# Turning the gated mixer sum and a quarter of the normed rows by transposing DMAs in a two-layer encoder kernel

## The chip, the cores and the metric

The kernel runs on one core of a Trainium2 chip. The metric is the device time of one launch in microseconds. Before the change it was 1870.2 us, the median of three runs (1869.01 to 1872.32).

## The reference, cut to what matters

Two layers, each a half-step FFN, a gated mixer and a second half-step FFN; a final RMSNorm. D is 1024, there are 512 tokens, the FFN is 2816 wide, everything is float32.

```python
def rms_norm(x, g):
    return x * rsqrt(mean(x * x, -1) + 1e-6) * g
def swiglu(x, w_in, w_out):                       # w_in 1024 x 5632, w_out 2816 x 1024
    g, u = split(x @ w_in, 2)
    return (silu(g) * u) @ w_out
def mixer(h, ...):
    q, k, v, uf, ga, gf = columns_of(h @ w_in)
    y_na = neighbourhood_attention(q, k, v, rpb) @ w_na_out
    y_f = fourier_mix(uf) @ w_f_out               # real part of a 2-D DFT
    g_na, g_f = sigmoid(ga + bias[0]), sigmoid(gf + bias[1])
    return (g_na * y_na + g_f * y_f) @ w_o        # the gated mixer sum, times w_o
for l in range(2):
    x = x + 0.5 * swiglu(rms_norm(x, ffn1_norm[l]), ffn1_w_in[l], ffn1_w_out[l])
    x = x + mixer(rms_norm(x, mix_norm[l]), ...)
    x = x + 0.5 * swiglu(rms_norm(x, ffn2_norm[l]), ffn2_w_in[l], ffn2_w_out[l])
out = rms_norm(x, final_norm)
```

## The kernel before, in words

**Engines.** PE is TensorE, DVE is VectorE, ACT is ScalarE, POOL is GpSimd, SP is SyncE; a queue named after an engine holds the DMAs that this engine issues, in order.

**Products.** Each float32 factor is split into a high and a low part of the multiplying type, and a product is three matmuls per block, high times high, high times low and low times high (`late_low`, L491, L492 and L494). The large products are also cut into 2x2 blocks and formed by Strassen's seven products, which carry the numbers 1 to 7 in the code; sums of blocks are needed on both sides. PE multiplies with the activations as the stationary operand (128 channels on the partitions by 128 tokens), so activations must stand with channels on the partitions: what is computed with tokens on the partitions is turned (transposed) first.

**Weights.** They stream from HBM in pieces (granules) of 128x1024 float32, 512 KB. SP loads a piece into a `raw` buffer (L148). Where Strassen needs a sum of two pieces, it is formed in one of two ways: DVE adds two loaded buffers (L164), or POOL issues a second DMA that accumulates onto the loaded buffer (L150; L196 for a buffer that has been used and becomes the sum). Then ACT copies the high part, `whi` (L191, L186 where the sign is turned), and DVE subtracts for the low part, `wlo` (L194, L187). `whi` and `wlo` have three buffers each. A product asks for its pieces two ahead (`AHEAD`), and loading runs eight pieces ahead of splitting (`FETCH`); in an FFN `raw` has nine buffers of its own, in a mixer its buffers come from the general pool of 23 slots. The order of instructions on each engine is made by a scheduler from the order of the program, except in stretches under `manual_schedule`, where the program's order is kept. Each engine runs its instructions strictly in that order, SP and POOL too.

**FFN.** After the gate and up products come 21 steps (`steps` in `stage_ffn`), each one Strassen product of an activation block with pieces of the out-projection: first product 1 with the three chunks of the inner width (steps 0 to 2), then product 2 (3 to 5), then products 5, 6, 7, 3 of chunk 0 (6 to 9), of chunk 1 and of chunk 2, then product 4. DVE forms the activation sums (`at`, L742) and their low parts (`c5l` and so on, L322); ACT makes the high parts (`c5h`, L321). Products go to PSUM banks `o`; finished ones are added into the residual `x` (`update`, L748).

**How the FFN turns its activations.** `halves` (L676) lets ACT copy the low and the high 16 bits of a 128x1024 float32 block apart into `zs` (two copies, L681); SP then issues a transposing DMA from `zs` to `zt` (L682). `joined` (L687) later lets ACT put the two halves together in `at` (L698). This runs ten times in each FFN, while the gate and up products are being made.

**How the residual rows are turned.** The next block needs the normed rows with channels on the partitions: `Norm.quad(i, j)` turns the quarter of `x` with channels `i*512` and up and tokens `j*256` and up. `quad_high` (L385) issues eight PE transposes of 128x128 float32 into two PSUM banks named `tr` (L396), ACT copies them out in four pieces and multiplies each by its gain, which goes by channel and so by partition (`xr`, L399), then makes the high part `xh` (L400); DVE makes the low part `xl` (L401). In the three FFNs that are not the last one (`late` is false), the quarter (0, 0) is turned in step 6 (L942), when product 2 has been added to it; two more are turned in the step of product 4 with chunk 0.

**The mixer's gated sum.** `gate_block(0, ...)` and `gate_block(1, ...)` (L1374) form the two column halves of the gates by seven products each, in the order 1, 5, 2, 6, 7, 3, 4, with banks `A`, `B` and `C`; ACT copies finished banks out (`snap`, L561, tile `sn`), and `after` is a table of what else is done behind which product. Block 0 leaves the finished gated sum of the first 512 channels in `ga0[0]` and `ga0[1]` (tiles `fs`, 256 tokens each). During block 1, `to_channels(0, ga0, 1)` behind product 5 and `to_channels(0, ga0, 0)` behind product 2 turn these: eight PE transposes each (L1462) into two banks `tr`, two ACT copies to `mq` (L1463). Then come the products with `w_o` ("wA" to "wC"), which read `mq`; the second half of the sum is turned at their start by `to_channels(1, ...)`.

Of the kernel before, what the change touches and what calls it, by code (L numbers as in the profile page):

```python
# [9 lines left out]
F32 = mybir.dt.float32  # L10
# [3 lines left out]
U16 = mybir.dt.uint16  # L14
AF = mybir.ActivationFunctionType
# [3 lines left out]
P = 128  # L19
D = 1024  # L20
T = 512
# [69 lines left out]
def encoder_kernel(  # L91
    ctx: ExitStack, tc: tile.TileContext, xin, xtr, wst, gains, gfin, gbias, bias_in, dft, chan, ident_in, rot, out
):
    nc = tc.nc
    V, S, G, PE = nc.vector, nc.scalar, nc.gpsimd, nc.tensor
# [11 lines left out]
    def nm(s):  # L107
        uid[0] += 1
        return f"{s}_{uid[0]}"

    def slot(dt=F32, s="k", shape=(4, 256)):
        return kp.tile([P, *shape], dt, tag="k", name=nm(s), bufs=23)
# [8 lines left out]
    def pair(s="ps"):  # L121
        return [bank(s), bank(s)]


    x = cp.tile([P, TB, D], F32, tag="x", name="x")
# [193 lines left out]
    def split(hi, lo, src, scale=None):  # L319
        if scale is None:  # L320
            S.activation(hi, src, AF.Copy)  # L321
            V.tensor_tensor(lo, src, hi.bitcast(F32), ALU.subtract)  # L322
            return
        S.activation(hi, src, AF.Copy, scale=scale)
        V.scalar_tensor_tensor(lo, src, scale, hi.bitcast(F32), ALU.mult, ALU.subtract)
# [5 lines left out]
    def rsqrt(ms, n):  # L331
# [6 lines left out]
            V.scalar_tensor_tensor(r, t, 1.5, r, ALU.add, ALU.mult)  # L338
        return r

    class Norm:


# [37 lines left out]

        def quad(self, i, j):
            self.quad_high(i, j)()

        def quad_high(self, i, j):  # L385

# [211 lines left out]
    def stage_ffn(norm, nxt, late):  # L598
# [4 lines left out]
        def at_tile(h, j, c):  # L603
            if (h, j, c) not in at:
                at[h, j, c] = slot(F32, "at")
            return at[h, j, c]
# [17 lines left out]
        raw = norm.raw  # L624
# [17 lines left out]
        acts, steps_of = combos(norm, t4)  # L642
# [6 lines left out]
        if first:  # L649
            for g in range(2):  # L650
                w = ws.next()
# [22 lines left out]
        late_at, turned = [], []  # L674

        def halves(z, j, f0):  # L676

            s, t = slot(U16, "zs", (2, 4, 2, P)), slot(U16, "zt", (2, 4, 256))
            words = z.bitcast(U16).rearrange("p b (q f h) -> p h q b f", q=4, h=2)
            for h in range(2):  # L680
                S.activation(s[:, h], words[:, h], AF.Copy)  # L681
            nc.sync.dma_start_transpose(  # L682
                out=t.rearrange("p h q (b t) -> p (h q b) t", b=2), in_=s.rearrange("p h q b f -> p (h q b f)")
            )
            turned.append((t, j, f0))

        def joined():  # L687

            t, j, f0 = turned.pop(0)
            q = 0  # L690
            while q < 4:
                h, c, i = PLACE[f0 + q]
                n = 1
                while q + n < 4 and PLACE[f0 + q + n] == (h, c, i + n):
                    n += 1
                to = at_tile(h, j, c).bitcast(U16).rearrange("p i (t w) -> p w i t", w=2)
                for w in range(2):
                    S.activation(to[:, w, i : i + n, :], t[:, w, q : q + n, :], AF.Copy)  # L698
                q += n

        def plain_out():
# [161 lines left out]
        for jb in range(0 if first else 1, NB):  # L863
            f0 = 2 + 4 * jb
            if first and jb == 0:
                with tc.manual_schedule(engines={mybir.EngineType.DVE, mybir.EngineType.Activation}):
                    pa = pair("A")
                    product(pa, acts[1], K4, True)
                    for j in range(2):
                        t = snap(pcl[j])  # L870
# [39 lines left out]
        for i, (m, c, _) in enumerate(steps):  # L910
            make(i)
            if i:
                make(i + 1)
            key = {6: 1, 4: 7}.get(m, m)
            if key not in ps:
                ps[key] = pair(f"o{key}")
            if m == 4 and c == 0 and nxt.mix:
                make(i + 2)
                ws.finish_stage()
                swap_pools(1)  # L920
            product(
                ps[key], made.pop(i), list(range(len(CHUNK[0][c]))), c == 0 and m in (1, 2, 3, 5, 7), c == 2,
                m in (4, 6), by_block=late and i == len(steps) - 1,
            )
            if i == 0:
                settle_at()
            if i == 2:
                turned.reverse()
                joined()
            if i == 5:  # L930
                joined()
            if m == 4 and c == 0 and not late:
                with tc.manual_schedule(engines={mybir.EngineType.DVE, mybir.EngineType.Activation}):
                    make(i + 2)
                    nxt.quad(1, 1)
                    if nxt.mix:
                        nxt.low01 = nxt.quad_high(0, 1)
                    else:
                        nxt.quad(0, 1)
            make(i + 2)  # L940
            if i == 6 and not late:
                nxt.quad(0, 0)  # L942
            if m == 4 and c == 1:
                update(ps[1], 1, 0, 1)
            if m == 4 and c == 0 and late:
                gf[0] = slot(F32, "gf", (D,))
                nc.sync.dma_start(out=gf[0], in_=bass.AP(tensor=gfin.tensor, offset=gfin.offset, ap=[[0, P], [1, D]]))
            if c < 2:
                continue
            if m == 1:  # L950
                update(ps[1], 0, 0, -1)
            elif m == 2:
                update(ps[2], 0, 0, 1)
                nxt.squares(0, 0)
            elif m == 5:
                update(ps[5], 0, 1, 1)
                update(ps[5], 1, 1, -1)
            elif m == 6:
                update(ps[1], 1, 1, 1)
            elif m == 7:  # L960
                update(ps[7], 1, 1, 1)
                nxt.squares(1, 1)
                update(ps[1], 0, 1, -1)
            elif m == 3:
                update(ps[3], 0, 1, 1)
                nxt.squares(0, 1)
                if late:
                    make(i + 3)
            elif late:
                with (  # L970
                    tc.issue_after(ws.items[-1].last.ins),
                    tc.manual_schedule(engines={mybir.EngineType.DVE, mybir.EngineType.Activation}),
                ):
                    ready = nxt.inverses(2)
                    next(ready)
                    gained(2, 0)
                    next(ready)
                    gained(2, 1)
                    for _ in ready:
                        pass  # L980
                    scaled(nxt, 2)
                    update(ps[7], 1, 0, 1, (0,))
                    nxt.squares(1, 0, (0,))
                    root = [nxt.inverse(b, *nxt.terms(b)) for b in range(2)]
                    next(root[0])
                    gained(3, 0)
                    gained(3, 1)
                    scaled(nxt, 3)
                    update(ps[7], 1, 0, 1, (1,))
                    nxt.squares(1, 0, (1,))  # L990
                    next(root[1])
                    next(root[0])
                    gained(0, 0)
                    next(root[0])
                    gained(0, 1)
                    scaled(nxt, 0)
                    next(root[1])
                    next(root[1])
                    whole(nxt, 1, 0)
                    whole(nxt, 1, 1)  # L1000
            else:
                update(ps[7], 1, 0, 1)
                if not nxt.mix:
                    nxt.squares(1, 0)
                nxt.later((1, 0))
# [29 lines left out]
    def stage_mixer(l, norm, nxt):  # L1035
# [219 lines left out]
        o, q, k, bms = [], {}, {}, {}  # L1255
# [197 lines left out]
        mq = {}  # L1453

        def to_channels(i, ga, j):
            mq[i, j] = slot(F32, "mq")
            for q in range(2):
                tr = bank("tr").rearrange("p (a b) -> p a b", a=2)
                for k in range(2):
                    for b in range(2):  # L1460
                        d = (2 * q + k) * P
                        PE.transpose(tr[:, k, b * P : (b + 1) * P], ga[j][:, b, d : d + P], ident)  # L1462
                S.activation(mq[i, j][:, 2 * q : 2 * q + 2, :], tr, AF.Copy)  # L1463
# [26 lines left out]
        with tc.manual_schedule(engines={mybir.EngineType.DVE, mybir.EngineType.Activation}):  # L1490
            with tc.manual_schedule(engines={mybir.EngineType.PE}):
# [29 lines left out]
                f0, f1 = four_ch(b_[0]), four_ch(b_[1])  # L1521
# [30 lines left out]
                for s in range(3):  # L1552
                    t = slot(F32R, "vs", (2, T))
# [142 lines left out]
        acts = {1: (hx[0], lx[0], 0), 2: (hx[1], lx[1], 0), 3: (hx[1], lx[1], 256), 4: (hx[0], lx[0], 256)}  # L1696
# [11 lines left out]
        with tc.manual_schedule(engines={mybir.EngineType.DVE, mybir.EngineType.Activation}):  # L1708
# [10 lines left out]
            w = [ws.next(), ws.next()]  # L1719
        for _ in fill(o, ns, 0, w):  # L1720
            pass
        bias = []
# [20 lines left out]

        ga0 = gate_block(0, bias, acts, {1: third_parts, 6: fourth})

        ga1 = gate_block(1, bias, acts, {5: lambda: to_channels(0, ga0, 1), 2: lambda: to_channels(0, ga0, 0)})
        m00, m01 = mq[0, 0], mq[0, 1]
        a1 = parts(m00, "m1")
        a5 = combo(m00, m00, m01, ALU.subtract, "m5")
        w = [ws.next(), ws.next()]  # L1750
# [86 lines left out]
    for l in range(L):  # L1837
        nxt = Norm(3 * l + 1)
        stage_ffn(norm, nxt, False)
        norm, nxt = nxt, Norm(3 * l + 2)  # L1840
        stage_mixer(l, norm, nxt)
        norm, nxt = nxt, Norm(3 * l + 3)
# [141 lines left out]
```

## Time and profile before

| what | us |
|---|---|
| median of three runs | 1870.2 |
| lowest, highest | 1869.01, 1872.32 |
| profiled execution | 1872.91 |
| its span in the trace | 1871.1 |
| PE busy | 1854.5 |
| DVE busy | 1638.3 |
| ACT busy | 1307.7 |
| POOL busy | 171.4 |

The span goes from the first to the last event of the trace; the rest of the execution's time lies around it. The granted clock of TensorE was 0.999 of full speed. HBM was read at 197 GB/s over the span. In the trace's rows a start comes first, in us from the span's start, then a duration; "x4" is the number of like instructions that the row takes together; what stands in brackets at the end is how long the engine sat idle before and what ended that. A group's row gives minimum, median and maximum of one instruction's duration in ns, and the starts of the first and last.

### The profile page before, as it was taken

The page shows a single profiled execution, that of the slowest core. Times are in us where ns is not written, and L with a number is a line of the kernel's source. Part 1 is how long each engine was busy: PE and PEld are TensorE (multiplying, and loading weights), DVE is VectorE, ACT ScalarE, POOL GpSimd, SP SyncE. Part 2 cuts the span into 40 slices and gives each one's busy share as a digit, 9 for nine tenths or more (in the row PEclk, how much of TensorE's full clock was granted, in tenths as well). Part 3 has the DMA queues.
Part 4 walks back from the last instruction along what each step waited for, and adds up shares of the span by engine and source line. Part 5 has one row for each costly group of instructions (what it writes and reads, how often), then busy time and mean ns, then how long its engine had stood idle before and what let it go on. Part 6 is the DMA issues. An engine that isn't in the chain of part 4 may idle for free.

```text
span 1871.1 us, 24628 instructions
## 1 busy us (share of the span) xinstructions
PE 1854.5 (99%) x8830; PEld 1543.7 (82%) x8830; DVE 1638.3 (88%) x2006; ACT 1307.7 (70%) x1788; POOL 171.4 (9%) x210
## 2 busy tenths in 40 slices
PE   9999999999999999999999999999999999999998
PEld 7888878888888888888888888878887888888886
DVE  7877899788989987889998888997889899888899
ACT  6777875668666867777666778666685567677865
POOL 0001011100111001001010100101001101010010
PEclk9999999999999999999999999999999999999999
DMA  9898798932886888879888887988248867888794
GB/s 302 223 236 210 196 255 271 230 103 90 248 219 161 179 225 225 223 195 259 259 196 220 225 219 200 269 266 202 85 139 229 213 166 176 221 227 222 196 283 151
DMA packets 190139, 393.70 MB, mean 210 GB/s; under 512 B 95488, under 2 KB 95616, under 8 KB 190016
## 3 DMA queue, kind: packets, MB, share of 16 engines
q1 hardware_dynamic: 161344, 293.77, 48.8%
q0 software_dynamic: 28528, 98.33, 29.6%
q8 instruction: 69, 1.13, 0.2%
q14 instruction: 54, 0.44, 0.1%
q10 hardware_dynamic: 144, 0.02, 0.0%
HBM read 365.85 MB, written 2.11 MB: 197 GB/s over the span
## 4 chain that ended last, share of the span: by engine, by line
PE 85%; DVE 5%; DMA 5%; issue 4%; ACT 1%; POOL 0%; SPq 0%; DVEq 0%; ACTq 0%; POOLq 0%
PE A L491 10%; PE A L492 10%; PE A L494 10%; PE B L492 5%; PE B L491 5%; PE B L494 5%; PE o L494 5%; PE o L492 5%; PE o L491 5%; DMA raw<-in_wst_dram 4%; PE ps L315 3%; PE ps L316 3%; PE ps L317 3%; PE C L491 2%; PE C L492 2%
## 5 line engine op out<-in xcount | busy, mean ns | idle before, releaser
L194 DVE TENSOR_TENSOR wlo<-raw,whi 128x1024 fp32r<-128x1024 f32 (+1 forms) x534 | 630.8, 1190 | 165.6 <-ACT whi L191 164.2
L191 ACT ACTIVATE whi<-raw 128x1024 fp32r<-128x1024 f32 (+1 forms) x534 | 547.2, 1033 | 270.5 <-DVE raw L164 59.8
L150 POOL DMA_DIRECT2D raw<-in_wst_dram x166 | 144.3, 889 | 1337.4 <-DMA raw<-in_wst_dram 895.5
L164 DVE TENSOR_TENSOR raw<-raw,raw 128x1024 f32<-128x1024 f32 (+1 forms) x150 | 178.5, 1191 | 2.0
L492 PE MATMUL A<-whi,xl 128*128 128x512 f32 x400 | 155.7, 389 | 0.0
L491 PE MATMUL A<-whi,xh 128*128 128x512 f32 x400 | 155.7, 389 | 0.0
L698 ACT ACTIVATE at<-zt 128x1024 uint16<-128x1024 uint16 (+2 forms) x96 | 111.0, 1168 | 20.6 <-DMA zt<-zs 20.6
L186 ACT ACTIVATE whi<-raw 128x1024 fp32r<-128x1024 f32 (+1 forms) x83 | 85.9, 1035 | 50.2 <-PE A L492 13.6
L494 PE MATMUL A<-wlo,xh 128*128 128x512 f32 x400 | 115.0, 389 | 0.0
L187 DVE SCALAR_TENSOR_TENSOR wlo<-raw,whi 128x1024 fp32r<-128x1024 f32 (+1 forms) x83 | 98.2, 1192 | 12.9 <-ACT whi L186 12.8
L494 PEld LDWEIGHTS A<-wlo,xh 128*128 128x128 f32 x400 | 75.1, 188 | 15.6
L491 PEld LDWEIGHTS A<-whi,xh 128*128 128x128 f32 x400 | 75.1, 188 | 15.4
L492 PEld LDWEIGHTS A<-whi,xl 128*128 128x128 f32 x400 | 75.1, 188 | 15.4
L491 PE MATMUL C<-whi,xh 128*128 128x512 f32 x208 | 81.3, 391 | 0.5 <-ACT whi L191 0.5
L492 PE MATMUL C<-whi,xl 128*128 128x512 f32 x208 | 81.0, 389 | 0.0
L492 PE MATMUL B<-whi,xl 128*128 128x512 f32 x208 | 81.0, 389 | 0.0
L491 PE MATMUL B<-whi,xh 128*128 128x512 f32 x208 | 80.9, 389 | 0.0
L681 ACT ACTIVATE zs<-th 128x1024 uint16<-128x1024 uint16 x80 | 79.5, 1042 | 0.9 <-DVE th L729 0.9
L722 ACT ACTIVATE th<-sn,rh 128x512 f32<-128x512 f32 x80 | 55.1, 715 | 35.4 <-DVE sn L566 34.6
L561 ACT ACTIVATE sn<-A 128x512 f32<-128x512 f32 x104 | 59.1, 585 | 23.6 <-PE A L494 23.6
L494 PE MATMUL C<-wlo,xh 128*128 128x512 f32 x208 | 59.8, 389 | 0.0
L494 PE MATMUL B<-wlo,xh 128*128 128x512 f32 x208 | 59.8, 389 | 0.0
(449 smaller groups left out, 4772.0 us busy)
## 6 DMA issues: line engine op xcount, KB each, us to landing
raw<-in_wst_dram SPq DMA_DIRECT2D x470, 512.0 KB, 5.7
raw<-in_wst_dram POOLq DMA_DIRECT2D x174, 512.0 KB, 8.0
raw<-in_wst_dram SPq DMA_DIRECT2D x30, 256.0 KB, 3.5
bm<-in_bias_dram SPq DMA_DIRECT2D x16, 384.0 KB, 3.8
vs<-v SPq DMA_DIRECT2D x12, 256.0 KB, 3.8
x<-in_xin_dram SPq DMA_DIRECT2D x4, 512.0 KB, 10.2
raw<-in_wst_dram POOLq DMA_DIRECT2D x8, 256.0 KB, 8.4
dft<-in_dft_dram POOLq DMA_DIRECT2D x8, 256.0 KB, 4.3
```

Source lines behind the costliest of these rows:

```text
L150: G.dma_start(out=self.t, in_=wst[GRAN_AT[self.plus]][:, 0 : self.n], accum_op=ALU.add)
L164: V.tensor_tensor(self.raw.t, self.raw.t, self.add.t, ALU.add)
L186: S.activation(hi, t, AF.Copy, scale=-1.0)
L187: self.last = V.scalar_tensor_tensor(lo, t, -1.0, hi.bitcast(F32), ALU.mult, ALU.subtract)
L191: S.activation(hi[:, cs], t[:, cs], AF.Copy)
L194: self.last = V.tensor_tensor(lo[:, cs], t[:, cs], hi[:, cs].bitcast(F32), ALU.subtract)
L491: PE.matmul(ps, lh, rh, start=start, stop=False, skip_group_check=again)
L492: PE.matmul(ps, ll, rh, start=False, stop=False, skip_group_check=again)
L494: PE.matmul(ps, lh, rl, start=False, stop=stop, skip_group_check=again)
L561: S.activation(t[:, b, :], ps[b], AF.Copy)
L681: S.activation(s[:, h], words[:, h], AF.Copy)
L698: S.activation(to[:, w, i : i + n, :], t[:, w, q : q + n, :], AF.Copy)
```

## The change

Two places are turned by the FFN's way instead of by PE. The steps of `halves` and `joined` become the helpers `apart` and `joined_words` (the FFN's own turning is the same as before). A new `Norm.quad_apart(0, 0)` replaces `quad(0, 0)` in step 6 of the three FFNs: it copies the halves apart and issues the transposing DMA, and returns `rest`, which is called in step 9: it joins the halves in `xr`, multiplies by the gains in place in four passes, and makes `xh` and `xl`. In both mixers the two calls `to_channels(0, ...)` are replaced: `apart` for `ga0[1]` behind product 1 of block 1 and for `ga0[0]` behind product 5, and the joining into `mq` behind products 2 and 7. `to_channels(1, ...)` and all other turnings stay.

```diff
+    def apart(z):
+        s, t = slot(U16, "zs", (2, 4, 2, P)), slot(U16, "zt", (2, 4, 256))
+        words = z.bitcast(U16).rearrange("p b (q f h) -> p h q b f", q=4, h=2)
+        for h in range(2):
+            S.activation(s[:, h], words[:, h], AF.Copy)
+        nc.sync.dma_start_transpose(
+            out=t.rearrange("p h q (b t) -> p (h q b) t", b=2), in_=s.rearrange("p h q b f -> p (h q b f)")
+        )
+        return t
+
+    def joined_words(to, t):
+        to = to.bitcast(U16).rearrange("p i (t w) -> p w i t", w=2)
+        for w in range(2):
+            S.activation(to[:, w], t[:, w], AF.Copy)
...
+        def quad_apart(self, i, j):
+            t = apart(x[:, 2 * j : 2 * j + 2, i * T : (i + 1) * T])
+            def rest():
+                self.tiles(i)
+                js = slice(j * 256, (j + 1) * 256)
+                raw = self.raw[i, j] = slot(F32, "xr")
+                joined_words(raw, t)
+                for k in range(4):
+                    S.activation(raw[:, k, :], raw[:, k, :], AF.Copy, scale=self.gain(4 * i + k))
+                split(self.h[i][:, :, js], self.l[i][:, :, js], raw)
+            return rest
...
             if i == 6 and not late:
-                nxt.quad(0, 0)
+                rest00 = nxt.quad_apart(0, 0)
+            if i == 9 and not late:
+                rest00()
...
-        ga1 = gate_block(1, bias, acts, {5: lambda: to_channels(0, ga0, 1), 2: lambda: to_channels(0, ga0, 0)})
+        turned = {}
+
+        def taken(j):
+            turned[j] = apart(ga0[j])
+
+        def channels(j):
+            mq[0, j] = slot(F32, "mq")
+            joined_words(mq[0, j], turned[j])
+
+        ga1 = gate_block(
+            1, bias, acts, {1: lambda: taken(1), 5: lambda: taken(0), 2: lambda: channels(1), 7: lambda: channels(0)}
+        )
```

More of the change, by code (lines that the diff above doesn't have):

```diff
@@ L676, in halves @@
         def halves(z, j, f0):
[L678 to L685, printed above, removed]
+            turned.append((apart(z), j, f0))
         def joined():
@@ L695, in joined @@
                     n += 1
-                to = at_tile(h, j, c).bitcast(U16).rearrange("p i (t w) -> p w i t", w=2)
-                for w in range(2):
-                    S.activation(to[:, w, i : i + n, :], t[:, w, q : q + n, :], AF.Copy)
+                joined_words(at_tile(h, j, c)[:, i : i + n, :], t[:, :, q : q + n, :])
                 q += n
```

## The prediction

> **What bounds the kernel now.** I read the page first, then the groups of the tiles that the edit touches, then busy time by stretches, then the timelines of those places.
>
> ```profile
> span 1871.1 us, 24628 instructions
> PE 1854.5 (99%) x8830; PEld 1543.7 (82%) x8830; DVE 1638.3 (88%) x2006; ACT 1307.7 (70%) x1788; POOL 171.4 (9%) x210
> ```
>
> PE does nothing else for 99% of the span, so work taken from PE can be worth its full length, but only where nothing else ends there. The profiled execution took 1872.91 us, 1.81 more than its span and 2.7 more than the median 1870.2; the sum is a difference against this execution, and goes onto the median.
>
> The windows (us; then busy time and instructions of PE, PEld, DVE, ACT and POOL; granted clock; DMA share; GB/s) show two kinds of place: three stretches in the out-products that end an FFN, and one in the mixer.
>
> ```profile
> 260.00:300.00 40.00, 39.69 (x175) 32.32 (x174) 39.73 (x38) 24.46 (x26) 5.16 (x6) 1.00 1.03 294
> 870.00:900.00 30.00, 30.00 (x134) 24.82 (x134) 29.93 (x28) 17.38 (x19) 5.16 (x6) 1.00 1.04 322
> 1190.00:1220.00 30.00, 30.00 (x132) 24.32 (x132) 27.48 (x26) 15.87 (x17) 5.12 (x6) 1.00 1.03 320
> 530.00:550.00 20.00, 20.00 (x97) 16.58 (x96) 14.34 (x15) 12.48 (x16) 1.72 (x2) 1.00 0.79 217
> ```
>
> In the FFN tails DVE is as full as PE (39.73 of 40.00, 29.93 of 30.00) and DMA is at or over its capacity; in the mixer DVE has 14.34 of 20.00 and ACT 12.48, and only PE is full. The clock is 1.00 in all four.
>
> **What PE loses.** The instruction order of the changed program lacks 56 PE transposes: 8 for `quad(0, 0)` in three FFN tails, 16 for `to_channels(0, ...)` in two mixers. They are seven groups of eight.
>
> ```profile
> L396 PE MATMUL tr<-ident,x x160: 270/272/273, 257.0 to 1559.3; 128*128 128x128 f32 x160
> L1462 PE MATMUL tr<-ident,fs x32: 270/272/273, 533.7 to 1468.8; 128*128 128x128 f32 x32
> ```
>
> ```profile
> 533.66 1.03 PE L1462 MATMUL tr<-ident,fs 128*128 128x128 f32 x8
> 534.45 0.48 PE L491 MATMUL C<-whi,xh 128*128 128x512 f32 x1
> 534.77 0.40 PE L492 MATMUL C<-whi,xl 128*128 128x512 f32 x1
> 535.00 0.39 PE L491 MATMUL C<-whi,xh 128*128 128x512 f32 x1
> ```
>
> Matmuls overlap, so starts count: 534.77 to 535.00 is the ordinary pitch, 0.23. From 533.66 to 534.77 lies one ordinary matmul and the group: 1.11 - 0.23 = 0.88 us. Seven groups make 7 x 0.88 = **6.2 us, 0.33%**: the most that this edit can bring.
>
> **What it adds.** Per group: two 16-bit copies on ACT, one transposing DMA on SP's queue, two joining copies on ACT. In an FFN tail four gain scalings move from PSUM reads to in-place SBUF passes. The kernel does these steps already:
>
> ```profile
> L698 ACT ACTIVATE at<-zt x96: 477/1358/1378, 83.6 to 1780.6; 128x1024 uint16<-128x1024 uint16 x64, 128x256 uint16<-128x256 uint16 x16, 128x768 uint16<-128x768 uint16 x16
> L682 SPq DMA_TRANSPOSE zt<-zs x40: 1424/3460/7362, 72.6 to 1764.1; - x40
> DMA to landing us min/median/max: 4.3/5.6/10.9
> L681 ACT ACTIVATE zs<-th 128x1024 uint16<-128x1024 uint16 x80 | 79.5, 1042 | 0.9 <-DVE th L729 0.9
> L1463 ACT ACTIVATE mq<-tr x16: 576/590/601, 535.0 to 1509.2; 128x512 f32<-128x512 f32 x16
> L399 ACT ACTIVATE xr<-tr,gn x80: 452/472/510, 258.2 to 1560.8; 128x256 f32<-128x256 f32 x80
> L1309 ACT ACTIVATE s<-s,rs x64: 492/495/511, 410.1 to 1391.5; 128x256 f32<-128x256 f32 x64
> ```
>
> ACT per mixer group: 2 x 1.04 + 2 x 1.36 - 2 x 0.59 = +3.6 us. Per tail the scalings cost 4 x 0.49 for 4 x 0.47, nearly nothing, so 2 x 1.04 + 2 x 1.36 = +4.8. The in-place gain scaling is not in the trace; its bounds are the PSUM read, 0.47, and the L1309 pass of the same shape, 0.50; I take 0.49. The row above shows what the new DMA costs its issuer: 3.46 us of SP's queue.
>
> [...] In the changed order the joining copies of the first tail stand behind the split that is now at 273.13:
>
> ```profile
> 273.13 1.07 ACT L191 ACTIVATE whi<-raw 128x1024 fp32r<-128x1024 f32 x1 [1.48 <-DVE raw L164]
> ```
>
> So by the trace's 5.6 the turned halves, asked for near 260.3 (below), are there 8 us before that. [...]
>
> **Mixers.** ACT's additions have room:
>
> ```profile
> 528.12 1.05 ACT L191 ACTIVATE whi<-raw 128x1024 fp32r<-128x1024 f32 x1
> 535.01 1.08 ACT L1463 ACTIVATE mq<-tr 128x512 f32<-128x512 f32 x2
> 540.76 1.06 ACT L1463 ACTIVATE mq<-tr 128x512 f32<-128x512 f32 x2
> 545.16 0.60 ACT L561 ACTIVATE sn<-A 128x512 f32<-128x512 f32 x1 [1.21 <-PE A L494]
> 547.04 0.58 ACT L561 ACTIVATE sn<-A 128x512 f32<-128x512 f32 x1
> ```
>
> ```profile
> 547.68 0.48 PE L491 MATMUL A<-whi,t3h 128*128 128x512 f32 x1
> ```
>
> The weight split made at 528.12 is first used by PE at 534.45 (the `C` row above): more than 5 us of lead, against 7.2 us of added ACT work spread over some 20 us of which 7.5 are idle. Nothing reads the turned halves until the next product. One place is tight: the second joining copies (1.36, pitch about 1.22) stand between the two snaps of `A` at 545.16 and 547.04; the second snap can then start at 545.16 + 0.47 + 1.22 = 546.85 and free its bank at 547.43, where PE, which asked for it at 547.68 and in the changed order asks two matmuls sooner, would take it near 547.2. Bounds: 0 (an empty lead elsewhere takes it up) to 0.4; I take 0.2 per mixer beside the gain of 2 x 0.88. Both mixers: 2 x (-1.76 + 0.2) = -3.1, between -3.5 and -2.7. Each transposing DMA delays weight loads on SP by 3.5 us, but DMA is at 0.79 here and they were issued early.
>
> **FFN tails.** Here PE already waits for DVE, and DVE for DMA through ACT:
>
> ```profile
> 265.65 0.50 PE L494 MATMUL o<-wlo,c7h 128*128 128x512 f32 x1 [0.31 <-DVE wlo L194]
> 1238.56 1.21 PE L494 MATMUL o<-wlo,c3h 128*128 128x512 f32 x4 [0.69 <-DVE wlo L194]
> 281.27 2.01 ACT L191 ACTIVATE whi<-raw 128x1024 fp32r<-128x1024 f32 x2 [1.77 <-DMA raw<-in_wst_dram]
> 282.36 1.23 DVE L194 TENSOR_TENSOR wlo<-raw,whi 128x1024 fp32r<-128x1024 f32 x1 [0.27 <-ACT whi L191]
> 896.47 1.06 ACT L191 ACTIVATE whi<-raw 128x1024 fp32r<-128x1024 f32 x1 [0.25 <-DMA raw<-in_wst_dram]
> 1208.75 2.01 ACT L191 ACTIVATE whi<-raw 128x1024 fp32r<-128x1024 f32 x2 [2.03 <-DMA raw<-in_wst_dram]
> 1209.85 1.23 DVE L194 TENSOR_TENSOR wlo<-raw,whi 128x1024 fp32r<-128x1024 f32 x1 [1.68 <-ACT whi L191]
> ```
>
> Taking 0.88 us from PE brings it sooner to a split that DVE cannot make sooner. Replayed by hand in the new order, with transfers where they were, the tails come out at +0.2, -0.1 and 0.0 us: the gain is gone, because DVE has no slack and because joining copies and scalings push a few `whi` splits by 1.5 us.
>
> To this comes d, the delay of weight pieces that POOL accumulates onto SP's loads. In the first tail:
>
> ```profile
> 258.24 1.55 ACT L399 ACTIVATE xr<-tr,gn 128x256 f32<-128x256 f32 x4
> 260.41 0.33 SPq L148 DMA_DIRECT2D raw<-in_wst_dram  x1
> 261.55 0.93 SPq L148 DMA_DIRECT2D raw<-in_wst_dram  x2
> DMA to landing us min/median/max: 4.1/7.6/8.7
> 269.79 0.86 POOL L150 DMA_DIRECT2D raw<-in_wst_dram  x1 [10.19 <-DVE at L742]
> 271.14 0.86 POOL L150 DMA_DIRECT2D raw<-in_wst_dram  x1 [0.49 <-DVE wlo L194]
> ```
>
> The 16-bit copies take the place at 258.24 and end near 260.3. The transpose stands on SP ahead of the load at 260.41 and holds SP until 263.8; the two loads at 261.55 and 262.15 then go near 264.1 and 264.4, 2.5 and 2.3 late. They land 7.6 us later (the landing row is of SP's loads from 255 to 285): 271.7 and 272.0. The first accumulation then goes 1.9 us late, the second between 0.9 (its own load's landing) and 1.9 (its distance to the first kept), and the second is what ACT awaits at 281.27. Bounds for d: 0 (landing times vary from 4.1 to 8.7, the queueing may swallow the slip) and 3.5 (the whole 3.46 of the row). I take 1.8, near the upper of these two. What is left of lead in the replay is 0.3 us in the first tail, 0.7 in the second, 0.2 in the third: 1.5 + 1.1 + 1.6 = 4.2, with 0.1 from above 4.3.
>
> **Sum.** -3.1 + 4.3 = +1.2 us: 1874.1 against the profiled 1872.9, and **1871.4** on the median. At d = 0 it is -3.0 (1867.2); at d = 3.5 it is -3.1 + 0.1 + 3.2 + 2.8 + 3.3 = +6.3 (1876.5). A measurement of this kernel tells about 0.2%, 3.7 us, from no change.
>
> **Rivals.**
> 1. The tails keep their gain: lead elsewhere in DVE's queue is larger than I replayed, and d is 0. Then up to 6.2 us go: 1864.0; at half the tails' gain, -3.1 - 1.3, 1865.8. For it: PE waits only 0.31 and 0.69 in the rows above. Against: DVE 39.73 of 40.00. [...] No row here shows a transpose beside POOL's accumulations.
> 2. Slower: the transpose in the full DMA stretch delays the accumulated weights by the whole issue time. Beyond d = 2.7 the sum, -3.0 + 3d - 1.2 us, passes +3.7; at 3.5 it is +6.3, 1876.5. Place: `whi` splits like those at 281.27 and 1208.75, whose DMA waits grow from 1.77 and 2.03 towards 5. For it: DMA shares of 1.03 and waits already there. Against: the loads' own lead.
> 3. ACT blocked in order by a late transpose in a mixer: at the maximum landing of 10.9 the joining copies hold it 5.3 us longer than planned, as much as the lead of `whi`; worth 0 to +3, 1870 to 1873.
> 4. The transposes were not on the path in the mixers either: only +4.3 remains, 1874.5. Against: PE is 20.00 of 20.00 there without a wait.
>
> **How the numbers follow.** Forecast (d from 0.3 to 2.7, or rival 3): 0.46. Rival 1: 0.23. Rival 2: 0.26. Rival 4: 0.05. Faster by over 0.2% is rival 1 without its mildest part, 0.22; slower is rivals 2 and 4, 0.31; same 0.47. The forecast's own range is 1867.5 to 1874; the 8-in-10 range takes in half the tails' gain and d up to 3.5: 1865.5 to 1877.
>
> **What would show it.** Right: PE 56 instructions fewer; mixers shorter by 1.5 us each; tails no shorter, with longer waits of `whi` on DMA. Wrong: tails shorter by 0.9 each with DVE idle nowhere (rival 1), or DVE idle 3 us and more per tail (rival 2).

## The result, and the profile after

The changed kernel took 1881.05 us, the median of four runs (1880.8 to 1883.59), against 1870.36 us before: 10.7 us slower, a ratio of 1.0059 with a 95% interval of 1.0042 to 1.0077. The forecast was 1871.4, no change, and the range ended at 1877. In a later comparison the same kernel took 1889.08 against 1869.46, 1.0102 (1.0087 to 1.0117): the loss itself differs from one measurement to the next.

The page of the changed kernel's profile, its totals and its chain of waits:

```profile
span 1879.0 us, 24559 instructions
PE 1853.9 (99%) x8774; PEld 1538.1 (82%) x8774; DVE 1637.5 (87%) x2006; ACT 1331.5 (71%) x1808; POOL 171.4 (9%) x210
PE 86%; DVE 6%; DMA 3%; ACT 2%; issue 2%; SPq 0%; DVEq 0%; POOL 0%; ACTq 0%; POOLq 0%
```

PE has 56 instructions fewer, as the order said, and DVE's work is the same; yet the span is 7.9 us longer. The same four stretches as in the prediction show where PE now stands still:

```profile
260.00:300.00 40.00, 37.31 (x157) 28.71 (x156) 35.54 (x34) 25.36 (x30) 5.16 (x6) 1.00 1.05 289
870.00:900.00 30.00, 27.98 (x116) 22.50 (x115) 24.79 (x24) 19.71 (x23) 3.44 (x4) 0.94 1.05 283
1190.00:1220.00 30.00, 28.23 (x121) 22.13 (x120) 25.60 (x26) 20.41 (x24) 5.12 (x6) 1.00 1.06 272
530.00:550.00 20.00, 18.47 (x82) 15.01 (x81) 15.30 (x16) 17.02 (x21) 1.72 (x2) 1.00 0.90 188
```

In the first tail DVE, which had been full, is idle for 4.5 of 40 us; in the mixer, PE lost 1.5 of 20 us. To place it, I lined up the two traces by the k-th matmul of a product, transposes left out, and took the difference of their starts ahead of a stretch and behind it:

| stretch (start before, us) | change in the difference, us |
|---|---|
| first FFN tail, 250 to 345 | +3.84 |
| first mixer, 515 to 560 | -0.04 |
| second FFN tail, 855 to 945 | +4.77 |
| third FFN tail, 1175 to 1295 | +1.77 |
| second mixer, 1440 to 1520 | -0.25 |
| all the rest | -2.8 |

The rest lies where nothing was changed (single waits for weights near 161, 508 and 1436 that the trace of before had and this one has not). So the tails lost 10.4 us and the mixers gained 0.3 of the 3.1 forecast. One pair of traces is not exact in the tails: in four later kernels whose tails are as before (e1, e3, e10 and e11 below), the same three stretches differ from the trace of before by -0.2 to 2.1, by 0.0 to 1.9 and by -2.5 to -0.5 us. The first tail, queue by queue (SP, then POOL with the landing times of its two rows, then what ACT, DVE and PE wait for):

```profile
258.44 7.28 SPq L347 DMA_TRANSPOSE zt<-zs  x1
265.82 5.54 SPq L148 DMA_DIRECT2D raw<-in_wst_dram  x7
```

```profile
L150 POOL DMA_DIRECT2D raw<-in_wst_dram x2: 860/860/860, 256.7 to 257.9; - x2
...
DMA to landing us min/median/max: 6.1/6.9/7.7
```

```profile
272.23 0.86 POOL L150 DMA_DIRECT2D raw<-in_wst_dram  x1 [13.46 <-DVE wlo L194]
273.45 0.86 POOL L150 DMA_DIRECT2D raw<-in_wst_dram  x1 [0.36 <-DVE c6l L322]
```

```profile
284.87 1.06 ACT L191 ACTIVATE whi<-raw 128x1024 fp32r<-128x1024 f32 x1 [2.73 <-DMA raw<-in_wst_dram]
893.53 2.00 ACT L191 ACTIVATE whi<-raw 128x1024 fp32r<-128x1024 f32 x2 [1.39 <-DMA raw<-in_wst_dram]
1218.13 1.06 ACT L191 ACTIVATE whi<-raw 128x1024 fp32r<-128x1024 f32 x1 [2.75 <-DMA raw<-in_wst_dram]
```

```profile
285.96 1.23 DVE L194 TENSOR_TENSOR wlo<-raw,whi 128x1024 fp32r<-128x1024 f32 x1 [2.56 <-ACT whi L191]
```

```profile
278.15 0.50 PE L523 MATMUL o<-whi,c6h 128*128 128x512 f32 x1 [1.12 <-ACT whi L191]
282.19 0.50 PE L523 MATMUL o<-whi,c7h 128*128 128x512 f32 x1 [0.67 <-ACT whi L191]
285.98 0.50 PE L523 MATMUL o<-whi,c7h 128*128 128x512 f32 x1 [0.77 <-ACT whi L191]
```

The transposing DMA held SP for 7.28 us, not 3.46. It let go at 265.72, when the second of POOL's accumulating loads landed (257.9 + 7.7 = 265.6). Seven loads then leave within 5.5 us, the first at 265.82 where it had been 260.41. POOL's next accumulations, which had gone at 269.79 and 271.14, go at 272.23 and 273.45, in a trace that ran 0.87 us ahead until then; ACT waits for the second at 284.87 instead of 281.27, and DVE and PE wait for ACT. Not every stall of PE in the tail is of this chain. The first, 1.12 us at 278.15, is for a split that stands on ACT behind the four in-place scalings of the change, while the sum that it reads had been ready since 274.42:

```profile
275.46 1.69 ACT L412 ACTIVATE xr<-xr,gn 128x256 f32<-128x256 f32 x4
277.06 1.04 ACT L191 ACTIVATE whi<-raw 128x1024 fp32r<-128x1024 f32 x1
```

Of the three stalls, 1.12 us are thus ACT's own added work, and 0.67 and 0.77 late weights. In the second tail the long wait is one piece earlier, for the first of the two accumulations, and PE's only stall there, 2.02 us at 891.24, is for its split:

```profile
890.13 1.06 ACT L191 ACTIVATE whi<-raw 128x1024 fp32r<-128x1024 f32 x1 [5.16 <-DMA raw<-in_wst_dram]
```

The first mixer, with the second transposing DMA, its landing, and the three engines behind it:

```profile
537.91 4.51 SPq L347 DMA_TRANSPOSE zt<-zs  x1
```

```profile
DMA to landing us min/median/max: 9.8/9.8/9.8
```

```profile
547.72 1.34 ACT L356 ACTIVATE mq<-zt 128x1024 uint16<-128x1024 uint16 x1 [1.33 <-DMA zt<-zs]
548.93 0.56 ACT L593 ACTIVATE sn<-A 128x512 f32<-128x512 f32 x1
```

```profile
549.55 0.50 PE L523 MATMUL A<-whi,t3h 128*128 128x512 f32 x1 [1.53 <-ACT sn L593]
```

The half that the joining copy wants lands at 547.7; ACT stands before the copy for 1.33 us and is busy with it to 548.93, the snap of bank `A` stands behind it, and PE waits 1.53 us for the bank. That pays back the two groups of transposes.

### The profile page after: what moved, and what is told of

Its sections match the earlier page's. It is cut to its first block, busy times and chain, and to the rows that moved or that the text cites. A ratio compares the mean times of both kernels' runs of the same rounds, so it can differ in the third digit from the quotient of the medians.

```text
span 1879.0 us, 24559 instructions
## 1 busy us (share of the span) xinstructions
PE 1853.9 (99%) x8774; PEld 1538.1 (82%) x8774; DVE 1637.5 (87%) x2006; ACT 1331.5 (71%) x1808; POOL 171.4 (9%) x210
## 3 DMA queue, kind: packets, MB, share of 16 engines
q8 instruction: 69, 1.13, 0.2%
## 4 chain that ended last, share of the span: by engine, by line
PE 86%; DVE 6%; DMA 3%; ACT 2%; issue 2%; SPq 0%; DVEq 0%; POOL 0%; ACTq 0%; POOLq 0%
PE A L523 10%; PE A L526 10%; PE A L524 10%; PE B L524 5%; PE B L526 5%; PE B L523 5%; PE o L526 5%; PE o L524 4%; PE o L523 4%; PE ps L316 4%; PE ps L315 4%; PE ps L317 4%; PE C L523 2%; PE C L524 2%; PE C L526 2%; DMA raw<-in_wst_dram 2%
## 6 DMA issues: line engine op xcount, KB each, us to landing
x<-in_xin_dram SPq DMA_DIRECT2D x4, 512.0 KB, 10.2
```

## The experiments

The theory from these rows: a transposing DMA goes only when every transfer in flight has landed, holds its issuer until then, and the loads behind it on SP starve POOL's accumulations. The rivals: ACT's added work; 512 KB more in a full DMA stretch; and tails and mixers acting on each other.

**Each part alone.** The first edit takes the FFN tails back to PE, the second the mixers:

```diff
-                rest00 = nxt.quad_apart(0, 0)
-            if i == 9 and not late:
-                rest00()
+                nxt.quad(0, 0)
```

```diff
-            1, bias, acts, {1: lambda: taken(1), 5: lambda: taken(0), 2: lambda: channels(1), 7: lambda: channels(0)}
+            1, bias, acts, {5: lambda: to_channels(0, ga0, 1), 2: lambda: to_channels(0, ga0, 0)}
```

> The mixers' part alone; the FFN tails turn their quarter on PE as before. Theory (the loss is all in the tails, where the transposing DMA held SP's queue for 7.3 us; in the mixers the 1.78 us that PE saves is paid back by one stall, 1.69 us at 549.55, behind a snap of bank A that waits in ACT's order for a late transposed half): about -0.3 us, 1870.1 (1869 to 1871). Rival (the mixers give 3.1 us as predicted, and the stall came from weights that the tails had delayed): 1867.3.

> The FFN tails' part alone; the mixers turn their sum on PE as before. Theory: the three tails cost 4.2, 4.8 and 1.8 us as between the two traces, together +10.7: 1881.0 (1879.5 to 1882.5), with three transposing DMAs that hold SP over 7 us each. Rival (tails and mixers act on each other): under 1879.

Mixers alone: 1868.73 against 1870.21, 0.9990 (0.9981 to 0.9999). Tails alone: 1885.34, 1.0085 (1.0058 to 1.0111), above the range that I expected, with holds of 6.93, 7.66 and 7.68 us. So all of the loss is the tails', and the mixers alone bring a little, against my first reading: lined up as above, both mixers gained 1.48 and 1.45 us. The rival in the first expectation, that the mixers give what was predicted and lose it only beside the tails, was nearer.

**The mixers' joining later in the program**, behind product 3 instead of 7, without and with the tails (`7: lambda: channels(0)` becomes `3: lambda: channels(0)`), and the changed kernel once more beside it.

> The mixers' part alone, with the second joining put behind product 3 instead of product 7, so that it no longer stands between two snaps of bank A. Theory (the late half in ACT's order made the stall): the 1.7 us stall goes and both mixers keep 1.78 us: -3.5 us, 1866.9 (1866 to 1868). Rival (the transposing DMA on SP delays weight loads, and these stall PE): as the mixers' part alone, about 1870.

> The changed kernel with the second joining of the mixers put behind product 3 instead of product 7; tails as in the change. Theory (in the change the mixers' gain was lost in a snap of bank A that waits in ACT's order for a late half): the stall at the start of product 3 goes, and it is 1.5 to 3.5 us faster than the changed kernel of the same call. Rival (the mixers' loss is late weights): the same as the changed kernel.

> The changed kernel once more, for a second profile of it beside the next kernel. Theory: 9 to 12 us more than before; each tail's transposing DMA holds SP 6.5 to 7.7 us again and lands 2 us after the last transfer that was in flight at its issue. For the mixers: if the stall of 1.69 us at the snap of bank A is a matter of how the accumulating loads happen to lie, it comes out at another length; if it belongs to the order of the work, it is there again within 0.3 us.

Without the tails: 1868.38 against 1870.21, 0.9986 (0.9978 to 0.9995), in the trace again -1.48 and -1.45 us. With them 1890.14 against 1869.46, 1.0103 (1.0083 to 1.0124); the changed kernel itself 1889.08, 1.0102. The edit did nothing: the scheduler left ACT's joining between the two snaps of `A`, and every engine runs the same order as without it. With the tails, PE's stall there was 1.68 us with the edit and 1.58 in the repeat of the change. These two runs therefore test nothing about the joining; they are repeats of the mixers alone and of the change, and show that the stall comes back at nearly the same length when the tails are in.

The repeat of the change, which lost 19.6 us where I had expected 9 to 12, also shows a second, dearer form of the loss. In its second tail, an accumulating load of POOL and the transposing DMA were issued at the same time:

```profile
868.34 6.01 SPq L347 DMA_TRANSPOSE zt<-zs  x1
868.34 0.86 POOL L150 DMA_DIRECT2D raw<-in_wst_dram  x1 [0.59 <-DVE wlo L194]
```

```profile
DMA to landing us min/median/max: 18.5/18.5/18.5
```

```profile
886.98 1.06 ACT L191 ACTIVATE whi<-raw 128x1024 fp32r<-128x1024 f32 x1 [9.81 <-DMA raw<-in_wst_dram]
```

The load landed 18.5 us after its issue, the transpose 18.7, and ACT stood 9.81 us: this tail lost 12.9 us instead of 4.8. The transfers did not only wait for each other: from 874 to 886 us all of the core's DMA together moved 31 to 97 GB/s (in stretches of 2 us), against 178 to 248 from 866 to 870 and 365 from 886 to 888.

**The tails' turning later**, steps 13 and 17 instead of 6 and 9:

> The tails' part alone, seven and eight steps later: halves taken apart in step 13, joined in step 17. The ACT work and the DMA are the same. Theory (what costs is a transposing DMA put on SP's queue when DMA is full and accumulated weights come just in time): the stretch behind step 13 has a lower DMA share, so the hold of SP falls towards 3.5 us and the cost towards nothing: 1868.5 to 1873. Rival (ACT's 4.8 us more work, or DVE's fullness, whatever the DMA does): still 1878 or more.

1873.11 against 1870.21, 1.0013 (1.0004 to 1.0021). The cost falls from 15 to some 2.4 us, but not for the reason that I gave. The hold stays at 7.27, 6.73 and 6.95 us, and the stretch is no emptier:

```profile
293.02 7.27 SPq L347 DMA_TRANSPOSE zt<-zs  x1
```

```profile
285.00:300.00 15.00, 15.00 (x68) 12.43 (x67) 14.87 (x16) 9.83 (x10) 1.70 (x2) 1.00 1.09 266
```

PE is full there all the same. What differs is what follows: behind these three transposing DMAs POOL issues its next accumulating load only 21 to 25 us later (at 314.04, 924.68 and 1243.50), so no accumulation is waiting for the held loads just then. The rival, that ACT's work alone costs 8 us, falls.

**What of the tail costs.** Four kernels, in this order: the tails' part with the transposing DMA issued by ACT; the kernel before with only the DMA added; the kernel before with only ACT's four copies added; the tails' part with a plain DMA of the same bytes, which leaves the turning out.

```diff
-        nc.sync.dma_start_transpose(
+        q.dma_start_transpose(
...
-            t = apart(x[:, 2 * j : 2 * j + 2, i * T : (i + 1) * T])
+            t = apart(x[:, 2 * j : 2 * j + 2, i * T : (i + 1) * T], nc.scalar)
```

> The tails' part alone, with ACT instead of SP issuing the transposing DMA. Theory (a transposing DMA goes only when every transfer in flight, of either queue, has landed, and holds its issuer until then): ACT is held about 7 us in each tail, SP's loads are not, and the cost stays as ACT's splits come late: 1875 to 1886. Rival 1 (the transpose only waits for what stands before it on SP's own queue): on ACT's queue it holds under 3 us, and the tails cost nothing: 1868 to 1872. Rival 2 (only the hold of SP's loads costs, a held ACT does not): a hold of 7 us, and 1868 to 1873.

```diff
                 nxt.quad(0, 0)
+                idle = slot(U16, "zt", (2, 4, 256))
+                nc.sync.dma_start_transpose(
+                    out=idle.rearrange("p h q (b t) -> p (h q b) t", b=2), in_=x[:, 0, :].bitcast(U16)
+                )
```

> The kernel before, with one transposing DMA of the same size added on SP's queue in step 6 of the three FFNs, from residual rows into a buffer that nothing reads; PE still turns the quarter, ACT does nothing more. Theory (the transpose's hold of SP is the cost): three holds of 6.5 to 7.7 us, each equal to the time until the accumulating loads in flight have landed, and 8 to 16 us more: 1878 to 1886. Rival (ACT's 4.8 us more work per tail is the cost): 1870 to 1872.

```diff
                 nxt.quad(0, 0)
+                zs = slot(U16, "zs", (2, 4, 2, P))
+                words = x[:, 0:2, 0:T].bitcast(U16).rearrange("p b (q f h) -> p h q b f", q=4, h=2)
+                for h in range(2):
+                    S.activation(zs[:, h], words[:, h], AF.Copy)
+            if i == 9 and not late:
+                zr = slot(F32, "xr").bitcast(U16).rearrange("p i (t w) -> p w i t", w=2)
+                for w_ in range(2):
+                    S.activation(zr[:, w_], zs[:, w_].rearrange("p q b f -> p q (b f)"), AF.Copy)
```

> The kernel before, with the four 16-bit copies of a tail added on ACT (two in step 6, two in step 9, results unused) and no transposing DMA; PE still turns the quarter. Theory (the DMA's hold is the cost): 0 to 2 us more, 1870 to 1872.5. Rival (ACT's work is the cost): 1876 or more.

```diff
-            t = apart(x[:, 2 * j : 2 * j + 2, i * T : (i + 1) * T])
+            z = x[:, 2 * j : 2 * j + 2, i * T : (i + 1) * T]
...
+            for h in range(2):
+                S.activation(s[:, h], words[:, h], AF.Copy)
+            nc.sync.dma_start(out=t.rearrange("p h q t -> p (h q t)"), in_=s.rearrange("p h q b f -> p (h q b f)"))
```

> The tails' part alone, with a plain DMA of the same 512 KB from the separated halves to the same buffer in place of the transposing one; the rows are not turned, all else is the same. Theory (it is the transposing kind that waits for everything in flight): SP is held under 1 us, no weights are late, and the tails cost -1 to +3 us: 1869 to 1873. Rival (any 512 KB more in a stretch whose DMA share is 1.0 costs this): 1878 or more.

| kernel | us, against 1871.73 | ratio (95%) |
|---|---|---|
| issued by ACT | 1896.31 | 1.0152 (1.0105 to 1.0199) |
| DMA alone | 1882.36 | 1.0067 (1.0047 to 1.0087) |
| ACT's copies alone | 1874.08 | 1.0008 (0.9997 to 1.0018) |
| plain copy | 1875.34 | 1.0024 (1.0014 to 1.0034) |

The DMA alone costs about 12 us by the ratio (10.6 by the medians), ACT's copies alone too little to tell from nothing, and the plain copy, which holds SP for 0.54 us (the first row below), about a third of what the tails' part costs with the transposing one (1.0024 against 1.0085). The other two thirds are the transposing kind. The plain copy's third is more than I expected; its trace shows PE standing 1.13 us at 277.28 and 1.43 at 882.25, both times for a split that ACT makes behind the four scalings. That work is not in the kernel with ACT's copies alone, which keeps the scalings where they were. On ACT's queue the transposing DMA is worse, and dearer than I expected; the group of its row, its landing, and the instruction on ACT behind it:

```profile
257.55 0.54 SPq L409 DMA_DIRECT2D zt<-zs  x1
```

```profile
L347 ACTq DMA_TRANSPOSE zt<-zs x1: 9352/9352/9352, 257.8 to 257.8; - x1
...
DMA to landing us min/median/max: 13.5/13.5/13.5
```

```profile
267.30 0.63 ACT L191 ACTIVATE whi<-raw 128x512 fp32r<-128x512 f32 x1 [8.55 <-issue]
```

It held ACT 9.35 us, although nothing stood ahead of it on ACT's queue, and landed at 271.3. SP's three loads that were issued after it, from 258.9 to 260.6, take

```profile
DMA to landing us min/median/max: 8.0/8.8/9.1
```

and so had landed by 269.7: on another queue it landed behind later ones too. The rival of an own queue falls.

In the kernel with the DMA alone the holds were 3.78 to 4.64 us, shorter than I expected, and the landings 9.8 to 14.0. It waits for no copies, so it is issued some 2 us earlier than in the change, ahead of POOL's two accumulations instead of behind them. This kernel therefore does not price the hold of 7 us: lined up, its tails lost 2.6, 8.6 and 0.4 us, and the 8.6 is the dearer form again. There an accumulating load went 0.30 us behind the transposing DMA and landed after 13.7 us:

```profile
864.07 4.64 SPq L944 DMA_TRANSPOSE zt<-x  x1
864.36 0.86 POOL L150 DMA_DIRECT2D raw<-in_wst_dram  x1 [9.16 <-DMA raw<-in_wst_dram]
```

**Loads put in flight on purpose.** The mixers alone, where the first transposing DMA found nothing in flight; first one plain load on POOL's queue well ahead, then two, released by the first 16-bit copy (the edit of the second, cut):

```diff
+            if ahead and h == 0:
+                for g in range(2):
+                    d = slot(F32, "ahead", (1024,))
+                    S.activation(d.bitcast(U16)[:, 0:8], s[:, 0, 0, 0, 0:8], AF.Copy)
+                    G.dma_start(out=d, in_=wst[g][:, 0:1024])
...
-            turned[j] = apart(ga0[j])
+            turned[j] = apart(ga0[j], j == 1)
```

> The mixers' part alone, with one plain 512 KB load on POOL's queue into a buffer that nothing reads, put 1.5 to 3 us ahead of the first transposing DMA of each mixer, which in the mixers' part alone found nothing in flight, was held 2.0 and 1.4 us and landed after 5.9 and 4.5. Theory (a transposing DMA goes only when all in flight has landed, whatever its queue): its hold grows to the time until that load has landed, 3 to 5 us, and its own landing comes 2 us after that of the load. Rival (only its own queue counts): hold 2.0 and 1.4 us as before.

> The mixers' part alone, with two plain 512 KB loads on POOL's queue into buffers that nothing reads, released by the first 16-bit copy of each mixer, so that they are in flight when the first transposing DMA is issued about 1 us later. Theory (a transposing DMA goes only when all in flight has landed, whatever its queue): it is held 4 to 7 us instead of 2.0 and 1.4, and lands 2 us after the last of the two loads. Rival (only its own queue counts): hold 1.4 to 2.0, landing 4.5 to 6.

The first (one execution, 1873.62 us) told nothing apart: the load had landed 1.2 us after the transpose's issue, and the hold of 2.39 us has room for both readings. With two, SP and POOL in the first mixer:

```profile
531.21 5.25 SPq L352 DMA_TRANSPOSE zt<-zs  x1
```

```profile
530.44 1.15 POOL L351 DMA_DIRECT2D ahead<-in_wst_dram  x2 [8.44 <-DVE fs L1418]
```

```profile
DMA to landing us min/median/max: 3.8/4.7/5.6
```

The hold went from 2.02 to 5.25 us and ends at 536.46, as the second load lands (issued at 531.05, 5.6 later: 536.66). The load on POOL's queue, which nothing waits for, holds SP. In the second mixer the hold stayed at 1.36 us, as the rival had it, but the transpose landed after 7.3 us, 2.0 behind the second load. One execution of this kernel took 1897.52 us: in both mixers the next transposing DMA and POOL's accumulations landed 13.9 to 18.6 us after that DMA's issue.

**The joining really moved**, by putting it into the manual order behind both snaps of `A` and the tanh, without and with the tails:

```diff
                         with_n(arg(s1, 0, 0), 0)
+                        if "snapped" in after:
+                            after["snapped"]()
...
-            1, bias, acts, {1: lambda: taken(1), 5: lambda: taken(0), 2: lambda: channels(1), 7: lambda: channels(0)}
+            1, bias, acts, {1: lambda: taken(1), 5: lambda: taken(0), 2: lambda: channels(1), "snapped": lambda: channels(0)}
```

> The mixers' part alone, with the second joining kept on ACT behind both snaps of bank A and the gate's tanh by a manual order; moving its place in the program had left ACT's order as it was. Theory (a snap that queues behind the joining holds PE): the 0.3 us stall per mixer that was left goes, -3.2 us, 1867 against 1870 of before. Rival (the split that now stands between the snaps waits for an accumulated weight piece and holds the second snap instead): a stall of 0.3 to 1 us stays, and 1868 to 1869.5.

> The changed kernel with the same manual order of the second joining; tails as in the change. Theory (in the change the first mixer's gain is lost in a snap of bank A queued behind a joining that waits for a late half): the stall of 1.5 to 1.7 us at the start of product 3 falls under 1 us. In time it can hardly be told, since the tails scatter by more: 1879 to 1892. Rival (something else holds the bank): the stall stays at 1.5 to 1.7.

With the tails the stall at the start of product 3 falls to 0.24 us and the first mixer gains 1.35 us instead of 0.04, which shows its cause:

```profile
548.22 0.50 PE L523 MATMUL A<-whi,t3h 128*128 128x512 f32 x1 [0.24 <-ACT sn L593]
```

The whole kernel stays slow, 1891.01 against 1869.88, 1.0106 (1.0064 to 1.0149): in two of its tails an accumulating load met the transposing DMA and landed after 17.0 and 21.1 us. Without the tails it took 1867.35, 0.9984 (0.9975 to 0.9993), the fastest here, though its trace shows the rival's stall (1.05 us, a split of a late weight piece between the snaps); it can't be told from the mixers alone.

## Why the prediction was wrong, point by point

The sum was +1.2 us; lined up, the two traces differ by 7.3 at their end. The tails take 10.4 us instead of the 4.3 forecast, 6.1 more, the mixers 2.8 more than -3.1, and 2.8 less are spent where nothing was changed.

- **What PE loses**, 6.2 us at most: right, 56 instructions fewer.
- **Mixers**, -3.1 (-3.5 to -2.7): right by themselves, -2.93 in each of two traces. The place that I had named as tight was the one; its price was 0.2 and became about 1.7 in the first mixer, since the turned half landed 9.8 us after issue and not 5.6 (7.8 in the mixers alone; why it is later beside the tails is open). Rival 3 had this mechanism, at a landing of 10.9, but I counted it as one with the forecast. In the second mixer the gain went to a stall at the same snap (0.27 us beyond the pitch) and one for a `wlo` (0.90); these I have not traced further.
- **Tails without delay**, +0.1: too small. The plain copy, 1.0024, puts ACT's work and the bytes together at 4.5 us (2.6 to 6.4). I had seen that the scalings push a few splits by 1.5 us and took this to cost no more than the gain of the tail; the stalls of 1.13 and 1.43 us in that kernel's trace, and of 1.12 in the change's first tail, are such splits.
- **d, the step that failed.** I took the hold of SP from the median of its row, 3.46 us, and made it the upper bound for d too. The same row ends at 7.362, and 7.28, 7.30 and 7.34 is what the three tails had: the median is over forty DMAs, at 21 of which no load of POOL was in flight; the tails are where two accumulations are. The rows of before could have shown it, against my sentence that no row there has a transpose beside POOL's accumulations: 19 of the forty were issued beside one or two, and four of the five that held SP over 5 us had one with 5.9 to 7.5 us still to go.

Against the traces' lined-up clocks (-0.87, +2.37 and +7.13 us ahead of the three tails), the split that waits for the second accumulation came 4.5 us late in the first (284.87 for 281.27), 5.2 in the second (893.53 for the row below) and 2.3 in the third (1218.13 for 1208.75), where I had 1.8 and at most 3.5:

```profile
885.98 1.07 ACT L191 ACTIVATE whi<-raw 128x1024 fp32r<-128x1024 f32 x1 [1.53 <-DVE wlo L194]
```

In the first tail the steps are these: the two loads behind the transpose went 5.8 and 5.6 us late instead of 2.5 and 2.3, and landed 2.5 and 2.4 us sooner after their issue than before, so that the accumulations went 3.3 and 3.2 us late, and the second then took 11.3 us instead of 10.0.

Put into the sum that I had written down, d - 0.3, d - 0.7 and d - 0.2 beside the replay's 0.2, -0.1 and 0.0, these give 4.4, 4.4 and 2.1; the trace has 3.84, 4.77 and 1.77. So the chain from SP's hold to the late weights was right and its first duration was wrong. That the numbers agree so closely is partly luck: unchanged tails differ by up to 2.5 us between traces; part of the first tail's loss is ACT's; and in the second PE stood for the piece before (890.13 for 883.40, 4.4 us late), and the slower matmuls behind that stall cost another 1.6 us (last section).

- **Rivals.** Rival 2 was what happened, at its place and with its signs (waits on DMA in front of `whi`, DVE idle), but its price ended at d = 3.5. Rival 1 stood on d = 0, which no tail of the change shows: the splits came 4.5, 5.2 and 2.3 us late, and with two loads put in flight on POOL's queue the transposing DMA landed 3.2 and 2.0 us after the second of them.

That about two thirds of the tails' loss is the transposing kind is shown (1.0085 with it, 1.0024 with a plain DMA of the same bytes). Its two forms, loads held behind it on SP and the standstill at a meeting, are read from traces, and no run parts their prices. Why a hold sometimes ends early and the landing then comes late is not settled. Nor is why a load of POOL issued within 0.3 us ahead of it took 13.5 to 21.1 us in seven cases of fifteen, and one issued 0.14 to 0.34 us behind it 10.2 to 17.1 us in four of four; some of these are the FFN's own transposes, which the kernel before has too. Nor is why the changed kernel was 10.7 us slower in its first measurement and 19.6 in its second, and the tails alone 15, beyond that such meetings stand in several of the dearer traces.

## What to carry to other kernels

Before moving work to a transposing DMA, look at what is in flight, on every queue, where it will be issued: in these traces it landed after that (median 1.9 us after the last of it), and what stood behind it on its issuer was kept until the hold ended (7.28 us in the first tail of the change). Take a duration from the rows whose surroundings are those of the new place, not from the median of a group, and let the row's maximum bound the range. The group here went from 1.42 to 7.36 us and held several surroundings; sort the members of such a group by what else was in flight. Where the scheduler owns the order, see that a moved call has moved its instructions before reading anything from the time.

## What the runs showed of the hardware

- In the sixteen traces of this case are 700 transposing DMAs of 512 KB. None landed before the last transfer that was in flight at its issue; the median is 1.9 us after it. That order alone says little, since of 11221 plain transfers issued with something in flight only 653 landed ahead of it; the hold is what sets the kind apart. For 621 of the 700 the hold of the issuer is within 0.6 us of that time (or of 1.4 us, where less was left); a plain load's issue on SP takes 0.33 (the median in the trace of before). The fourteen with nothing in flight landed after 4.3 to 6.1 us, but those in the tails after 9.0 to 21.3, where the median of SP's loads from 255 to 285 us in the trace of before is 7.6.
- After PE had stood 2.02 us in the second tail, eight matmuls started 0.43 us apart instead of 0.23; by 895.61 PE had lost 1.6 us more. The granted clock was 0.50 from 893 to 895 us and 0.94 over the 30 us of that stretch. This stall and the slower matmuls behind it cost PE 3.6 us together.

```profile
891.24 0.50 PE L523 MATMUL o<-whi,c7h 128*128 128x512 f32 x1 [2.02 <-ACT whi L191]
892.62 0.63 PE L524 MATMUL o<-whi,c7l 128*128 128x512 f32 x1
893.05 0.63 PE L523 MATMUL o<-whi,c7h 128*128 128x512 f32 x1
893.48 0.63 PE L524 MATMUL o<-whi,c7l 128*128 128x512 f32 x1
```
